# Layer 1 of a two-layer trunk: keys, values and cached keys turned in 32 x 32 blocks by VectorE and placed by DMA

## The chip, the cores and the metric

The kernel runs on one core of one Trainium2 chip. The metric is the device time of one execution in microseconds (us), as the median of several runs. The core's engines work side by side, each through its own queue of instructions in order: TensorE (PE, with its weight loads shown apart as PEld), VectorE (DVE), ScalarE (ACT), GpSimd (POOL) and SyncE (SP). SP computes nothing here; it issues nearly all DMA transfers. An instruction waits at the head of its queue until the semaphores that it needs have come, and everything behind it in that queue waits too.

## What is computed

One inference step of a hybrid encoder trunk with two layers, for a prompt of 512 tokens and a sample of 32 tokens, 1024 wide. Layer 0 mixes tokens with RWKV-7, layer 1 with differential attention. The change is in layer 1, whose part of the reference is, cut down:

```python
h = rmsnorm(x, norm_w)
q, k, v, qm, gate = jnp.split(h @ w_in, [...], axis=-1)      # 12 heads of 128 for q, k and v
k_all = concat([k_past, k]); v_all = concat([v_past, v])     # sample only: 128 cached tokens
def probs(qa, ka):
    s = einsum('bqhd,bkhd->bhqk', qa, ka) * 64 ** -0.5
    return softmax(where(mask, s, NEG_INF))
attn = probs(q1, k1) - lam * probs(q2, k2)
o = einsum('bhqk,bkhd->bqhd', attn, v_all)
out = concat([rmsnorm(o, subln) * c, mem_attention(qm, mk, mv)]) * silu(gate)
return x + out @ w_out, k, v                                 # k and v are outputs too
```

Keys and values are needed in two layouts. The products give them transposed (features on the 128 partitions, tokens along the row). The outputs k and v, and the sum over `attn`, want tokens on the partitions. The cached keys come with tokens on partitions and are needed the other way for the sample's scores.

## The kernel before, in words

Prompt and sample are kept together as 544 columns, in two halves of 272. A main product is a matmul of 128 x 128 weights with 272 columns; weights and activations are split in a high and a low part (`whi`, `wlo`, `hh`, `hl`), so that one output column block of 128 takes 2 halves x 8 slices x 3 = 48 main products into `ps_g`. That is one **block** (`block`, `steps`). Weights come by DMA into five `raw` buffers, two loads for a block, and are split by ACT (`whi`) and DVE (`wlo`) one block ahead.

Layer 1 (`groups`) goes through twelve heads in three groups of four. Each head has a key block, a query block and a value block; after each group come gate blocks, and after the first two groups blocks for the memory's queries. All other work is dealt out among the main products: `block` takes a list of pieces, each with the number (0 to 47) of the main product ahead of which it is issued. The attention of one head is a generator (`diff_head`, `steps` inside it) of 13 pieces, which begin in the head's own value block and end in the next head's key and query blocks (for the group's last head: in a gate block and the block after it). `step(prev, 10, 20, 30, 40, 45)` puts the next five pieces of the previous head at products 10, 20, 30, 40 and 45.

The order within each engine's queue is made when the program is built: of the instructions that are ready at a point, the one that the code issues earlier goes first. In layer 1 no order is written by hand (`self.ordered` is False there).

The pieces of one head are, in order: the split of the keys in high and low (`kh`, `kz`; DMA moves half of `kh` to other partitions); the keys turned and written out; `scores(0)`, `scores(1)`; the sample's scores (`ps_sc`) and `probs(0)`; the values turned and written out; `scores(2)` and `probs(1)`; `weighted(0)`; `scores(3)`; `probs(2)`; `weighted(1)`; `weighted(2)`; `probs(3)`; `weighted(3)`. `scores(t)` makes the scores of 128 prompt tokens and their softmax on DVE and ACT, `probs(t)` turns the probabilities on PE (`ps_aT`), and `weighted(t)` sums t + 1 blocks of values on PE into `ps_o`. That tile comes from a pool of one bank (`psx`), and DVE copies it out to `ot`.

`turned` turns keys or values with four transposes on PE into `ps_kv`, ACT copies them to `kt` or `vt` in SBUF, and one DMA of 256 KB writes the output. For the sample's 32 tokens two more transposes (`ps_kvs`) and an ACT copy give `vs`. Once in a group, four transposes (`ps_ckT`) and an ACT copy turn the cached keys of four heads, which one DMA loaded to `ck`. `diff_end` ends a group: the sample's sums, and its outputs from `vs`. All of these instructions go through a queue object, so that the profile shows line 106 for them; they are told apart by tile.

Of the kernel before, what the change touches and what calls it, by code (L numbers as in the profile page):

```python
# [17 lines left out]
P = 128  # L18
# [90 lines left out]
class Trunk:  # L109
# [238 lines left out]
    def steps(self, w, evac):  # L348

        for v in (slice(0, TH), slice(TH, T)):  # L350
            if len(self.open) > 1:
                self.until(self.open.pop(0))
            ps = self.psg.tile([P, 512], F32, tag="g", name="ps_g")
            for k in range(KT):
                for t, x in ((0, self.hh), (0, self.hl), (1, self.hh)):
                    self.te.matmul(ps[:, :TH], w[t][:, k, :], x[:, k, v], start=k == 0 and x is self.hh and t == 0,
                                             stop=k == KT - 1 and t == 1)
# [1426 lines left out]
    def layer1(self):  # L1784
# [7 lines left out]
        with ExitStack() as ctx:  # L1792
            with ExitStack() as c2:
                self.dfp = p = self.pool("df", 1, ctx=c2)
                m1 = c2.enter_context(ExitStack())
                mp = self.pool("mem1a", 1, ctx=m1, side="right")

                nlam = self.nlam
                self.qs = [p.tile([P, P], F32, name=f"qs{i}") for i in range(2)]
# [98 lines left out]
    def groups(self, w, p, mp, nlam, aside, free):  # L1898

        late = []  # L1900
        for hg in range(3):
# [5 lines left out]
            def gate(c0, pieces):  # L1907
                self.gates += 1
                sg, _, evac = self.gate_evac(self.gates)
                self.block(w, 3 * MIXW + 512 + c0, evac, pieces)  # L1910
                return sg

            for j, (parts, it) in enumerate(heads):
                h = 4 * hg + j
                before = step(prev, 10, 20, 30, 40, 45) if j else late
                k, q, v = parts()
                self.block(w, MIXW + h * P, k, before)
                if not j and hg == 2:
# [12 lines left out]
            fin = lambda j, at: (at, lambda: end.send((j, sgs[j])))  # L1931
            g0 = 4 * hg * P
            sgs.append(gate(g0, step(prev, 10, 20, 30, 40, 45)))
            if hg == 2:
                sgs.append(gate(g0 + P, step(prev, 6, 18, 30, 42)))
                aside()
                sgs.append(gate(g0 + 2 * P, step(end, 2, 10, 18) + [fin(0, 22), fin(1, 36)]))
                sgs.append(gate(g0 + 3 * P, [fin(2, 16)]))
                fin(3, 0)[1]()
                break  # L1940
# [8 lines left out]
                    st["evac"](ps, v)  # L1949
                return evac  # L1950

            self.block(w, 3 * MIXW + st0["c"], query(st0), step(m0, 2) + step(prev, 6, 18, 30, 42))
# [16 lines left out]
    def diff_group(self, hg, p):  # L1969

        a, gr = self.a, {"hg": hg, "on": []}
        gr["ck"] = p.tile([P, 4, P], F32, tag="ck", name="ck")
        gr["cv"] = p.tile([P, 4, P], F32, tag="cv", name="cv")
        gr["ckT"] = p.tile([P, 4, P + TS], F32, tag="ckT", name="ckT")
        gr["vs"] = p.tile([TS, 2, 4, P], F32, tag="vs", name="vs")
        gr["ssb"] = p.tile([P, 2, 160], F32, tag="ssb", name="ssb")
        gr["ss"] = p.tile([P, 3, 16], F32, tag="oss", name="oss")
        return gr

    def cached(self, gr, n):  # L1980

        h = 4 * gr["hg"]
        self.se.dma_start(gr["c" + n][:], self.a["cache_" + n][0, 0, :, h : h + 4])

    def diff_head(self, gr, j, p, nlam):

# [28 lines left out]
            return keys, queries, values  # L2015

        def turned(x, n):
            t = p.tile([P, 4, P], F32, tag="kt" if n == 4 else "vt", name="kt" if n == 4 else "vt", bufs=n - 3)
            ps = self.psm.tile([P, 512], F32, tag="m", name="ps_kv")
            for i in range(4):  # L2020
                self.te.transpose(ps[:, i * P : i * P + P], x[:, i * P : i * P + P], self.ident[:])
            self.ae.copy(t[:], ps[:].rearrange("p (j c) -> p j c", j=4))
            self.se.dma_start(o[n][0, 0, :, h, :].rearrange("(i p) d -> p i d", p=P), t[:])
            return t

        def scores(t):
            n, S = (t + 1) * P, []
# [11 lines left out]
        def probs(t):  # L2039
            n = (t + 1) * P  # L2040
            ps = self.psm.tile([P, 512], F32, tag="m", name="ps_aT")
            for i in range(t + 1):
                self.te.transpose(ps[:, i * P : i * P + P], st["pt", t][:, 0, i * P : i * P + P], self.ident[:])
            st["aT", t] = p.tile([P, 512], F32, tag="aT", name="aT", bufs=2)
# [11 lines left out]
        def steps():  # L2056
# [8 lines left out]
            yield  # L2065
            turned(k, 4)
            if j == 0:
                ps = self.psm.tile([P, 512], F32, tag="m", name="ps_ckT")
                for i in range(4):
                    self.te.transpose(ps[:, i * P : i * P + P], gr["ck"][:, i, :], self.ident[:])  # L2070
                self.ae.copy(gr["ckT"][:, :, :P], ps[:].rearrange("p (j c) -> p j c", j=4))
            self.ae.copy(gr["ckT"][:, j, P:], k[:, TP:])
            yield
            scores(0)
# [8 lines left out]
            yield  # L2083
            if j == 0:
                self.cached(gr, "v")
            st["vt"] = turned(st["v"], 5)
            ps = self.psm.tile([P, 512], F32, tag="m", name="ps_kvs")
            for i, x in enumerate((k, st["v"])):
                self.te.transpose(ps[:, i * P : i * P + P], x[:, T - P :], self.ident[:])
            self.ae.copy(gr["vs"][:, :, j, :], ps[P - TS :, :256].rearrange("p (j c) -> p j c", j=2))  # L2090
# [23 lines left out]
    def diff_end(self, gr, nlam):  # L2114
# [4 lines left out]
        for i, n in ((0, 10), (1, 11)):  # L2119
            self.se.dma_start(o[n][0, 0, :, 4 * hg : 4 * hg + 4, :], vs[:, i])  # L2120
# [5 lines left out]
        aT = p.tile([P, 512], F32, tag="aT", name="aTs", bufs=2)  # L2126
        self.ae.copy(aT[:, :P], ps[:, :P])
        self.ae.copy(aT[:TS, P : 2 * P], ps[:TS, P : 2 * P])
        yield
# [4 lines left out]
                             tile_position=(0, 32 * j))  # L2134
        for j in range(4):
            rj = slice(32 * j, 32 * j + 32)
            self.te.matmul(po[rj, :P], aT[:TS, P + 32 * j : P + 32 * j + 32], vs[:, 1, j, :], start=False, stop=True,
                             tile_position=(0, 32 * j))
        os_ = p.tile([P, P], F32, tag="os", name="os")
        self.ve.tensor_copy(os_[:], po[:, :P])  # L2140
# [32 lines left out]
    def run(self):  # L2173
# [7 lines left out]
        self.ordered, self.later, self.open = False, [], []  # L2181
# [64 lines left out]
```

## Time and profile before

| What | Value |
|---|---|
| Median of 3 runs | 1370.9 us (1369.54 to 1371.71) |
| The profiled execution | 1371.42 us |
| Its span, first to last instruction | 1369.2 us |
| Granted TensorE clock, mean | 0.998 |
| Layer 1's heads and gates in the span | about 800 to 1250 us |
| Work on ps_kv, ps_kvs and ps_ckT | 132 matmuls on PE, 39 copies on ACT |

The times come from one profiled execution. A row of a group reads: line, engine, operation, tile written <- tiles read, shapes, count | busy time in us, mean ns of one | idle time of the engine ahead of them and who ended it. A row of a timeline reads: start in us, length in us, engine, line, operation, tiles, shapes, count. Rows that follow one another closely are merged, with their count at the end. Matmuls are pipelined, so their lengths overlap, and the price of one is read from the starts of its neighbours.

### The profile page before, as it was taken

Reading aid. Unit: us, or ns where it says so; the run is one execution under the profiler, and the core shown is the slowest. Engines: PE = TensorE matmul, PEld = TensorE weight load, DVE = VectorE, ACT = ScalarE, POOL = GpSimd, SP = SyncE. Lnnn points to the kernel's source line nnn. Section 1 sums busy time; section 2 is a strip of 40 time slices with the busy share of each in tenths; the row PEclk is TensorE's granted clock in tenths of the full one; section 3 lists DMA queues with packets and bytes.
Section 4 is the critical chain, followed back from the end, with each engine's and each line's share of the span. In section 5 each row is a group of like instructions: output and inputs, shape, how many; then the busy total and the mean of one; then the engine's idle time right before and its main releaser. Section 6 shows DMA issues by size and latency. Waiting matters only on the chain. (4 is left out here: it accounts for less than half of the span.)

```text
span 1369.2 us, 31861 instructions
## 1 busy us (share of the span) xinstructions
PE 1339.3 (98%) x11845; PEld 1283.9 (94%) x11845; DVE 939.7 (69%) x2353; ACT 822.6 (60%) x2288; POOL 381.9 (28%) x841
## 2 busy tenths in 40 slices
PE   8999999999999999999999999999999999999997
PEld 6988899999999998988999989999999999999997
DVE  5776788888888888667744667775567747667443
ACT  5766777877778777656433466654566537665222
POOL 2138667766686667600000120000000001002000
PEclk9999999999999999999999999999999999999999
DMA  7452322333323332432555563332333323332322
GB/s 224 146 140 70 77 71 57 94 86 74 88 67 84 88 88 64 142 87 76 173 142 147 148 184 88 100 102 82 101 95 94 90 82 94 97 97 79 93 78 73
DMA packets 276964, 139.06 MB, mean 102 GB/s; under 512 B 75769, under 2 KB 265730, under 8 KB 276810
## 3 DMA queue, kind: packets, MB, share of 16 engines
q1 hardware_dynamic: 276746, 137.01, 36.0%
q8 instruction: 94, 1.54, 0.5%
q14 instruction: 60, 0.49, 0.1%
q10 hardware_dynamic: 64, 0.02, 0.0%
HBM read 110.72 MB, written 22.91 MB: 98 GB/s over the span
## 5 line engine op out<-in xcount | busy, mean ns | idle before, releaser
L106 PE MATMUL ps_g<-hh,whi 128*128 128x272 f32 x1808 | 539.7, 299 | 1.0 <-DVE ats L106 0.7
L106 PE MATMUL ps_g<-hh,wlo 128*128 128x272 f32 x1808 | 534.8, 297 | 1.6 <-DVE wlo L106 1.5
L106 PE MATMUL ps_g<-hl,whi 128*128 128x272 f32 x1808 | 532.4, 295 | 0.6 <-DVE hl L106 0.3
L106 PEld LDWEIGHTS ps_g<-hh,whi 128*128 128x128 f32 x1808 | 341.2, 189 | 5.1 <-DVE ats L106 0.9
L106 PEld LDWEIGHTS ps_g<-hh,wlo 128*128 128x128 f32 x1808 | 340.6, 189 | 4.7 <-DVE wlo L106 2.5
L106 PEld LDWEIGHTS ps_g<-hl,whi 128*128 128x128 f32 x1808 | 341.1, 189 | 2.8 <-DVE hl L106 1.3
L106 DVE TENSOR_TENSOR wlo<-raw,whi 128x512 fp32r<-128x512 f32 x314 | 220.1, 712 | 118.3 <-ACT whi L106 114.7
L106 ACT CAST whi<-raw 128x512 fp32r<-128x512 f32 x314 | 188.9, 619 | 115.8 <-PE ps_g L106 62.4
L868 POOL TENSOR_TENSOR tm<-u,m 102x84 f32<-102x84 f32 (+23 forms) x341 | 147.8, 433 | 115.4 <-DMA m<-sc 69.5
L870 POOL TENSOR_TENSOR u<-u,tm 102x84 f32<-102x84 f32 (+23 forms) x341 | 151.6, 445 | 26.6
L106 PE MATMUL ps_g<-hi,wlo 128*128 128x272 f32 x512 | 147.8, 289 | 1.2 <-DVE wlo L106 1.2
L106 PE MATMUL ps_g<-hi,whi 128*128 128x272 f32 x512 | 147.7, 289 | 0.0
L106 PE MATMUL ps_g<-lo,whi 128*128 128x272 f32 x512 | 147.4, 288 | 0.0
L1339 POOL TENSOR_TENSOR lo<-og,hi 128x544 fp32r<-128x544 f32 x8 | 13.2, 1649 | 357.7 <-ACT hi L106 357.2
L106 PEld LDWEIGHTS ps_g<-hi,wlo 128*128 128x128 f32 x512 | 96.4, 188 | 1.7 <-DVE wlo L106 1.6
L106 PEld LDWEIGHTS ps_g<-hi,whi 128*128 128x128 f32 x512 | 96.5, 189 | 0.0
L106 PEld LDWEIGHTS ps_g<-lo,whi 128*128 128x128 f32 x512 | 96.4, 188 | 0.0
L106 ACT ACTIVATE pt<-ps_s,snm 128x128 f32<-128x128 f32 (+3 forms) x96 | 51.0, 532 | 41.7 <-DVE snm L106 41.6
L1763 POOL TENSOR_TENSOR hl<-hn,hh 128x544 fp32r<-128x544 f32 x8 | 12.2, 1536 | 211.4 <-ACT hh L106 211.3
L106 DVE SCALAR_TENSOR_TENSOR SB<-ps_c,dl,sd 64x64 f32<-64x64 f32 x168 | 47.4, 282 | 26.4 <-PE ps_c L106 21.2
L106 ACT COPY sv<-ps_c 64x64 f32<-64x64 f32 x192 | 39.6, 206 | 32.7 <-PE ps_c L106 30.8
L106 ACT ACTIVATE sg<-ps_g 128x272 f32<-128x272 f32 x64 | 25.2, 394 | 41.0 <-PE ps_g L106 38.3
(400 smaller groups left out, 2564.4 us busy)
## 6 DMA issues: line engine op xcount, KB each, us to landing
raw<-in_rw_in_dram SPq DMA_DIRECT2D x114, 256.0 KB
raw<-in_df_in_dram SPq DMA_DIRECT2D x112, 256.0 KB
raw<-in_w_out_dram SPq DMA_DIRECT2D x64, 256.0 KB
oscr<-sg SPq DMA_DIRECT2D x16, 272.0 KB
lo<-oscr SPq DMA_DIRECT2D x16, 272.0 KB
m<-sc SPq DMA_DIRECT2D x33, 128.0 KB
raw<-in_w_mem_v_dram SPq DMA_DIRECT2D x16, 256.0 KB
kh<-kh SPq DMA_DIRECT2D x24, 136.0 KB
```

The lines of the kernel that those rows point to most:

```text
L106: return lambda *a, **k: self.trunk.tie(self, issue(*a, **k))
L868: nc.gpsimd.tensor_tensor(tm[:, :n, :wd], u3[:, :n, kx : kx + 1].to_broadcast(sh), m3[:, kx : kx + 1, kx + 1 :].to_broadcast(sh), ALU.mult)
L870: nc.gpsimd.tensor_tensor(u3[:, :n, kx + 1 :], u3[:, :n, kx + 1 :], tm[:, :n, :wd], ALU.add)
L1339: (self.nc.gpsimd if g % 2 and self.o1 else self.ve).tensor_tensor(lo[:], t, hi[:].bitcast(F32), ALU.subtract)
L1763: nc.gpsimd.tensor_tensor(self.hl[:, k, :], h[:], self.hh[:, k, :].bitcast(F32), ALU.subtract)
```

## The change

DVE's transpose turns each 32 x 32 block of a tile by itself and leaves the blocks where they stand. The change uses it in place of PE's transposes, and lets DMAs put the blocks in place: 32 partitions at a time, in pieces of 32 numbers (128 B).

- **Keys**: one DVE transpose of 128 x 512 into `tb`, then four DMAs of 64 KB straight to the output. The last 32 columns are turned apart into `new`.
- **Values**: the same into `tb`, but four DMAs to a scratch tensor in DRAM (`vscr`, one for odd and one for even heads). Two pieces later (`fetched`) one DMA of 256 KB reads it back as `vt`; after `weighted(0)` another writes `vt` to the output.
- **The sample's keys and values**: from `new`, by four DMAs in a group to `vs` (`samples`) and four to the output.
- **Cached keys**: 16 DMAs, each a block column, in place of one, and four DVE transposes of 128 x 128 into `ckT`.
- **Order**: the pieces stand at products 4, 9, 30, 44 of the one block and 14, 24, 34, 46 of the next. `weighted(0)` moves from before `scores(3)` to after `probs(2)`, at product 14 of the query block; `weighted(1)` stands at 24, `weighted(2)` with `probs(3)` at 34, `weighted(3)` at 46.
- **Held places**: the first main product after a weighted sum may not be put ahead of it in PE's queue (`self.pinned`).
- `aT` has three buffers instead of two.

The diff, cut to its core:

```diff
@@ steps (main products) @@
+                    if self.pinned is not None:
+                        self.order(mm, self.pinned)
+                        self.pinned = None
@@ groups @@
-                before = step(prev, 10, 20, 30, 40, 45) if j else late
+                before = step(prev, 4, 9, 30, 44) if j else late
...
-                self.block(w, h * P, q, step(prev, 6, 18, 30, 42) if j else ())
+                self.block(w, h * P, q, step(prev, 14, 24, 34, 46) if j else ())
@@ cached @@
-        self.se.dma_start(gr["c" + n][:], self.a["cache_" + n][0, 0, :, h : h + 4])
+        if n == "v":
+            self.se.dma_start(gr["cv"][:], self.a["cache_v"][0, 0, :, h : h + 4])
+            return
+        for a in range(4):
+            for j in range(4):
+                r = slice(TS * a, TS * a + TS)
+                self.se.dma_start(gr["ck"][r, j].rearrange("i (b c) -> i b c", c=TS),
+                                  self.a["cache_k"][0, 0, :, h + j, r].rearrange("(b i) c -> i b c", i=TS))
@@ diff_head @@
         def turned(x, n):
-            t = p.tile([P, 4, P], F32, tag="kt" if n == 4 else "vt", name="kt" if n == 4 else "vt", bufs=n - 3)
-            ps = self.psm.tile([P, 512], F32, tag="m", name="ps_kv")
-            for i in range(4):
-                self.te.transpose(ps[:, i * P : i * P + P], x[:, i * P : i * P + P], self.ident[:])
-            self.ae.copy(t[:], ps[:].rearrange("p (j c) -> p j c", j=4))
-            self.se.dma_start(o[n][0, 0, :, h, :].rearrange("(i p) d -> p i d", p=P), t[:])
+            t = p.tile([P, TP], F32, tag="tb", name="kt" if n == 4 else "vb")
+            self.ve.transpose(t[:], x[:, :TP])
+            self.ve.transpose(gr["new"][:, n - 4, j, :], x[:, TP:])
+            to = o[4][0, 0, :, h, :] if n == 4 else self.vscr[h % 2][:]
+            to = to.rearrange("(b i) (a c) -> a i b c", i=TS, c=TS)
+            for a in range(4):
+                r = slice(TS * a, TS * a + TS)
+                self.se.dma_start(to[a], t[r, :].rearrange("i (b c) -> i b c", c=TS))
+
+        def fetched():
+            t = p.tile([P, 4, P], F32, tag="vt", name="vt", bufs=2)
+            self.se.dma_start(t[:], self.vscr[h % 2][:].rearrange("(i p) d -> p i d", p=P))
             return t
+
+        def samples():
+            for a in range(4):
+                r = slice(TS * a, TS * a + TS)
+                self.se.dma_start(gr["vs"][:, :, r], gr["new"][r, 1])
...
-                self.te.matmul(po[:, :P], aT[:, i * P : i * P + P], st["vt"][:, i, :], start=i == 0, stop=i == t)
+                self.pinned = self.te.matmul(po[:, :P], aT[:, i * P : i * P + P], st["vt"][:, i, :], start=i == 0, stop=i == t)
...
-            weighted(0)
-            yield
+            st["vt"] = fetched()
+            if j == 3:
+                samples()
             scores(3)
             yield
             probs(2)
             yield
+            weighted(0)
+            self.se.dma_start(o[5][0, 0, :, h, :].rearrange("(i p) d -> p i d", p=P), st["vt"][:])
+            yield
             weighted(1)
             yield
             weighted(2)
-            yield
             probs(3)
```

More of the change, by code (lines that the diff above doesn't have):

```diff
@@ L355, in steps @@
                 for t, x in ((0, self.hh), (0, self.hl), (1, self.hh)):
-                    self.te.matmul(ps[:, :TH], w[t][:, k, :], x[:, k, v], start=k == 0 and x is self.hh and t == 0,
-                                             stop=k == KT - 1 and t == 1)
+                    mm = self.te.matmul(ps[:, :TH], w[t][:, k, :], x[:, k, v], start=k == 0 and x is self.hh and t == 0,
+                                        stop=k == KT - 1 and t == 1)
+                    if self.pinned is not None:
+                        self.order(mm, self.pinned)
+                        self.pinned = None
                     if k == KT - 1 and t == 1:
@@ L1798, in layer1 @@
                 nlam = self.nlam
+                self.vscr = [self.dp.tile([TP, P], F32, name=f"vscr{i}") for i in range(2)]
                 self.qs = [p.tile([P, P], F32, name=f"qs{i}") for i in range(2)]
@@ L1932, in groups @@
             g0 = 4 * hg * P
-            sgs.append(gate(g0, step(prev, 10, 20, 30, 40, 45)))
+            sgs.append(gate(g0, step(prev, 4, 9, 30, 44)))
             if hg == 2:
-                sgs.append(gate(g0 + P, step(prev, 6, 18, 30, 42)))
+                sgs.append(gate(g0 + P, step(prev, 14, 24, 34, 46)))
                 aside()
@@ L1950, in query @@
                 return evac
-            self.block(w, 3 * MIXW + st0["c"], query(st0), step(m0, 2) + step(prev, 6, 18, 30, 42))
+            self.block(w, 3 * MIXW + st0["c"], query(st0), step(m0, 2) + step(prev, 14, 24, 34, 46))
             sgs.append(gate(g0 + P, step(end, 8, 20, 44)))
@@ L1974, in diff_group @@
         gr["ckT"] = p.tile([P, 4, P + TS], F32, tag="ckT", name="ckT")
-        gr["vs"] = p.tile([TS, 2, 4, P], F32, tag="vs", name="vs")
+        gr["vs"] = p.tile([TS, 4, P], F32, tag="vs", name="vs")
+        gr["new"] = p.tile([P, 2, 4, TS], F32, tag="new", name="new")
         gr["ssb"] = p.tile([P, 2, 160], F32, tag="ssb", name="ssb")
@@ L2067, in steps @@
             if j == 0:
-                ps = self.psm.tile([P, 512], F32, tag="m", name="ps_ckT")
                 for i in range(4):
-                    self.te.transpose(ps[:, i * P : i * P + P], gr["ck"][:, i, :], self.ident[:])
-                self.ae.copy(gr["ckT"][:, :, :P], ps[:].rearrange("p (j c) -> p j c", j=4))
+                    self.ve.transpose(gr["ckT"][:, i, :P], gr["ck"][:, i, :])
             self.ae.copy(gr["ckT"][:, j, P:], k[:, TP:])
@@ L2085, in steps @@
                 self.cached(gr, "v")
[L2086 to L2090, printed above, removed]
+            turned(st["v"], 5)
             st["ot"] = p.tile([P, 4, P], F32, tag="ot", name="ot", bufs=4)
@@ L2118, in diff_end @@
         self.combine(ssb, srs, P + TS, nlam)
-        for i, n in ((0, 10), (1, 11)):
-            self.se.dma_start(o[n][0, 0, :, 4 * hg : 4 * hg + 4, :], vs[:, i])
+        self.se.dma_start(o[11][0, 0, :, 4 * hg : 4 * hg + 4, :], vs[:])
+        for a in range(4):
+            r = slice(TS * a, TS * a + TS)
+            self.se.dma_start(o[10][0, 0, :, 4 * hg : 4 * hg + 4, r], gr["new"][r, 0])
         self.ve.tensor_scalar(ss[:, 1, :], ss[:, 0, :], 1.0 / P, EPS, ALU.mult, ALU.add)
@@ L2180, in run @@
         self.mem, self.out = {}, set()
-        self.ordered, self.later, self.open = False, [], []
+        self.ordered, self.later, self.open, self.pinned = False, [], [], None
         self.place_no = self.acted = 0
```

6 lines of the change are left out of this document (3 added, 3 removed).

## The prediction

> **What bounds the kernel now.** I read the page first, then busy time by window for layer 1, then TensorE's groups with shapes kept apart, then timelines of the stretch around one head.
>
> ```profile
> span 1369.2 us, 31861 instructions
> PE 1339.3 (98%) x11845; PEld 1283.9 (94%) x11845; DVE 939.7 (69%) x2353; ACT 822.6 (60%) x2288; POOL 381.9 (28%) x841
> ```
> ```profile
> 810.00:930.00 120.00, 119.87 (x961) 118.09 (x961) 84.75 (x252) 76.20 (x235) 0.00 (x0) 1.00 0.34 97
> 1141.00:1250.00 109.00, 109.00 (x878) 107.27 (x877) 77.52 (x235) 69.78 (x217) 0.15 (x2) 1.00 0.34 94
> ```
> The columns of the second are length, then busy time of PE, PEld, DVE, ACT and POOL, the granted clock, DMA share and GB/s. In the first and third group of heads PE never rests (119.87 of 120 us, 109.00 of 109) at full clock, while DVE has 71% of its time in use and the DMA engines 34%. In layer 1 time is therefore what PE must issue, plus whatever a change makes it wait.
>
> What PE would shed are these groups:
>
> ```profile
> L106 PE MATMUL ps_kv<-ident,k 128*128 128x128 f32 x48 | 7.2, 272 | 0.0
> L106 PE MATMUL ps_kv<-ident,v 128*128 128x128 f32 x48 | 7.2, 272 | 0.0
> L106 PE MATMUL ps_kvs<-ident,k 128*128 128x128 f32 x12 | 3.3, 273 | 0.0
> L106 PE MATMUL ps_kvs<-ident,v 128*128 128x128 f32 x12 | 3.3, 272 | 0.0
> L106 PE MATMUL ps_ckT<-ident,ck 128*128 128x128 f32 x12 | 1.8, 272 | 0.0
> ```
> That is 48 + 48 + 12 + 12 + 12 = 132 transposes. Their 272 ns is a latency, not a price, since matmuls overlap. The price is read from starts:
>
> ```profile
> 817.78 0.29 PE L106 MATMUL ps_g<-hl,whi 128*128 128x272 f32 x1
> ...
> 819.17 0.29 PE L106 MATMUL ps_g<-hh,whi 128*128 128x272 f32 x1
> 819.30 0.60 PE L106 MATMUL ps_kv<-ident,v 128*128 128x128 f32 x4
> ...
> 819.87 0.37 PE L106 MATMUL ps_g<-hl,whi 128*128 128x272 f32 x1
> 820.08 0.29 PE L106 MATMUL ps_g<-hh,wlo 128*128 128x272 f32 x1
> ```
> Eleven main products take 1.39 us, so one slot is 0.126 us. From 819.17 to 820.08 lie two such slots and six transposes: 0.91 - 0.25 = 0.66 us, or 0.110 us a transpose, entry and exit included.
>
> **The change, part by part.**
>
> *Transposes off PE.* 132 x 0.110 = 14.5 us, all of it on the path, since PE is what ends last there. Nothing else leaves PE: scores, weighted sums and their counts stay.
>
> *Transposes onto DVE.*
>
> ```profile
> L106 DVE STREAM_TRANSPOSE x<-xr x8: 735/738/739, 688.4 to 761.5; 128x544 f32<-128x544 f32 x8
> L106 DVE TENSOR_TENSOR og<-osT,sg 128x32 f32<-128x32 f32 x8 | 1.5, 183 | 0.0
> ```
> A 128x512 one is 512/544 of 738 ns, 0.69 us; for a 128x32 one I take the 0.18 us of the other row; a 128x128 one lies between them, near 0.3. Twelve heads with two long and two short ones, and three groups with four middling ones: 12 x 1.74 + 12 x 0.3 = 24 us, against 67 us that DVE rests in the two windows above alone. ACT loses its PSUM copies at the same time. Free as a total; its place is the question below.
>
> *The weighted sums.* This is the term that I can least pin down. They share one PSUM buffer (psx, one bank), so each waits until DVE has copied out the one before. For one head the trace shows:
>
> ```profile
> 848.76 0.38 PE L106 MATMUL ps_o<-vt,aT 128*128 128x128 f32 x2
> 853.25 0.61 PE L106 MATMUL ps_o<-vt,aT 128*128 128x128 f32 x4
> 855.19 0.83 PE L106 MATMUL ps_o<-vt,aT 128*128 128x128 f32 x6
> ```
> ```profile
> 853.95 0.27 DVE L106 COPY ot<-ps_o 128x128 f32<-128x128 f32 x1
> ...
> 854.73 0.68 DVE L106 TENSOR_TENSOR wlo<-raw,whi 128x512 fp32r<-128x512 f32 x1
> 855.33 0.74 DVE L106 SCALAR_TENSOR_TENSOR pt<-pt,srs 128x512 f32<-128x512 f32 x1
> 855.99 0.68 DVE L106 TENSOR_TENSOR wlo<-raw,whi 128x512 fp32r<-128x512 f32 x1
> 856.60 1.46 DVE L106 TENSOR_TENSOR kz<-k,kh 64x544 fp32r<-64x544 f32 x2
> 858.09 0.29 DVE L106 COPY ot<-ps_o 128x128 f32<-128x128 f32 x1
> ```
> The sum at 853.25 stands ahead of product 6 of the query block, so that block starts at 853.25 - 6 x 0.126 = 852.50. Its copy follows 0.1 us after it ends. The sum at product 18 ends at 856.02, and its copy comes 2.07 us later, because DVE first does work that the code issues earlier: weight split, softmax, the key's low parts, without a gap to 858.06. Today that lag costs nothing, the next sum being 24 products off. The change puts the first sum at product 14, the second at 24, the third at 34, and ties the following main product behind each, so PE can't run on: a late copy becomes a PE wait, with the whole block queued behind it.
>
> Bounds, in heads 1 to 3 of a group (nine in all; a group's last head is followed by gate and query blocks without the key's low parts, where I take no wait): the first sum starts 1.76 us into the block, ends 0.38 later at 2.14; the second is due at 24 x 0.126 + 0.22 = 3.24 (0.11 us for each of the first sum's two matmuls, as for a transpose). Copied at once: no wait. Copied only when the stretch ends, 858.06 being 5.56 us into the block: done at 5.9, wait 2.6 us. Interpolating the lag between product 6 (0.10) and 18 (2.07) gives 1.41 us at 14, copy done at 2.14 + 1.41 + 0.29 = 3.84, wait 0.6. And if the first copy slips in ahead, the second meets the stretch instead: the third sum is due at 34 x 0.126 + 0.67 = 4.95 and waits to 5.9, 0.9 us. I take 0.7 us a head, between the last two: 9 x 0.7 = 6.3 us given back.
>
> *The value's round trip.* SP's queue and its traffic in the same stretch, and a scratch write with its dependent read from layer 0:
>
> ```profile
> 844.00 0.38 ACT L106 COPY v<-ps_g 128x272 f32<-128x272 f32 x1
> ```
> ```profile
> 844.85 1.17 SPq L106 DMA_DIRECT2D raw<-in_df_in_dram  x2
> 846.11 0.46 SPq L106 DMA_DIRECT2D out_dram<-vt  x1
> 855.44 0.37 SPq L106 DMA_DIRECT2D raw<-in_df_in_dram  x1
> ```
> ```profile
> 844.80:845.80 1.00, 1.00 (x11) 1.00 (x10) 0.71 (x2) 0.59 (x2) 0.00 (x0) 1.00 0.00 0
> 847.80:848.80 1.00, 1.00 (x11) 1.00 (x10) 0.76 (x3) 1.00 (x4) 0.00 (x0) 1.00 1.06 312
> 850.30:855.40 5.10, 5.10 (x40) 4.93 (x40) 3.84 (x12) 3.39 (x9) 0.00 (x0) 1.00 0.00 0
> 752.40:753.40 1.00, 1.00 (x10) 1.00 (x9) 0.18 (x1) 0.00 (x0) 0.00 (x0) 1.00 0.73 113
> ```
> ```profile
> 113.54 1.83 SPq L106 DMA_DIRECT2D sc<-at  x4
> 115.47 0.40 SPq L106 DMA_DIRECT2D sc<-ats  x1
> 116.74 2.00 SPq L106 DMA_DIRECT2D sg<-sc  x6
> ```
> V is complete at 844.38 and can be turned by about 846.6, when SP's two loads are out too. Four writes at 0.46 us each: the last starts at 848.0. From the last scratch write to its reader took 116.74 - 115.47 = 1.27 us: the fetch starts at 849.3. Three transfers of 256 KB issued from 844.85 begin to move at 845.8 and are over by 850.3, so one takes 0.95 + 4.5/3 = 2.45 us: v is back at 851.8. The first sum would be due at 852.50 + 1.76, less the 0.88 us that the key block sheds (six transposes, and the first sum itself), 853.4. Spare: 1.6 us, and SP's next load (855.44) comes after it. Hidden, cost 0; uncovered it costs PE microsecond for microsecond in twelve heads. While SP waits for the writes only the output write and a load due 6 us later queue behind.
>
> The Trainium skill, "DMA: Bandwidth & Descriptors", section Specifications, speaks against the change: pieces below 512 B miss line rate. The last window above has 128 B pieces and moves 113 GB/s at a share of 0.73, where 512 B pieces moved 312 at 1.06, so the trace agrees: 1.9 times the engine time a byte. By that rule a head would need some 3 us more of all engines beside at least 18 us of main products (3 x 48 x 0.126), the DMA share going from 34% to at most 51%, which changes no term.
>
> *Cached keys in 16 transfers.*
>
> ```profile
> 803.35 1.28 SPq L106 DMA_DIRECT2D ck<-in_cache_k_dram  x1
> 806.53 1.13 SPq L106 DMA_DIRECT2D kh<-kh  x2
> ```
> ```profile
> 749.42 2.46 SPq L106 DMA_DIRECT2D xr<-in_x_prompt_dram  x4
> 812.71 0.22 PE L106 MATMUL ps_s<-kh,qp 128*128 128x128 f32 x1
> ```
> At 2.46/4 = 0.6 us an issue, 16 last 10 us in place of 1.28. For the first group they lie just ahead of the key's halves (806.53), which the first scores need at 812.71: between 0 and about 4 us once, if the halves go out 8.5 us later. For the other two groups they go into SP's idle time. I take 1 us.
>
> *The rest* (four transfers for the new keys, an aT buffer more, samples by DMA) goes to a queue and to memory that nothing here waits for: 0, the one buffer of turned keys and values being read out in about 4 us (four issues and a landing, by the rows above), while its next user comes 46 products, 5.8 us, later at the earliest.
>
> Sum: -14.5 + 6.3 + 1 = -7.2 us. The profiled execution took 1371.4 us (2.2 us outside its span), 0.5 above the median; 1370.9 - 7.2 = 1363.7 us.
>
> **The rivals.**
>
> *The copies always wait for the whole stretch* (slower). For it: DVE did all earlier-issued work first around 856 to 858, and the first sum ends just as the first split starts. Against it: the copy at 853.95 did slip between two softmax steps. Price: 9 x 2.6 = 23.4 us, -14.5 + 23.4 + 1 = +9.9: 1380.8 us. It decides from 1.5 us a head, (14.5 - 1)/9.
>
> *Full gain*: every copy finds a gap, as the one at 853.95 did, and the first load costs nothing: 1370.9 - 14.5 = 1356.4 us. Against it: 3.3 us without a gap on DVE.
>
> *Placing by DMA is too slow.* Small pieces double the round trip of 5.2 us (846.6 to 851.8) to 10.4; less 1.6 spare, 3.6 us a head, part of it the wait above: 12 x 3.6 = 43, 1370.9 - 13.5 + 43 = 1400 us; it breaks even at 1.1 us beyond the spare time. Against it: five writes of small pieces and their receipt took 3.2 us in layer 0. The Trainium skill, "VectorE: DVE Perf Modes", section The three transpose paths, warns that transposing by a plain DMA's strides is 19 times slower than the crossbar's way; by that it would be far worse than 1400. Here runs of 128 B stay whole, and the trace does not bear out such a factor.
>
> **How the numbers follow.** Forecast 0.36 (waits of 0.3 to 1.2 us a head: 1360 to 1368); whole stretch 0.32; full gain 0.23; slow DMA 0.09. A measurement of this kernel tells 0.2%, 2.7 us, from no change. Faster: 0.34 of the forecast and 0.22 of the full gain, 0.56. Slower: 0.27 of the whole stretch and 0.07 of the slow DMA, 0.34. Within 0.2%: 0.10. The range runs from the full gain, 1356.5, to the whole stretch, 1381; the tail of the DMA rival and a worse stretch are left out.
>
> **What would show it.** Right: no ps_kv, ps_kvs or ps_ckT; 132 matmuls fewer; twelve ps_o first sums without a wait for a DMA; some PE idle ahead of the second or third ps_o of a head, released by DVE's ot, 6 us in sum; ot copies behind kz. Wrong: that idle near 0, or above 13 us; PE or SP waiting on vscr; the first kh transfers several us later; PE's 0.126 us a product changed.

## The result, and the profile after

The changed kernel takes 1400.9 us (median of 4 runs, 1399.2 to 1402.2) against 1370.8 us before on the same chip (4 runs, 1369.5 to 1371.7): a ratio of 1.0220, 95% interval 1.0207 to 1.0232. The forecast was 1363.7 us, with a range to 1381. It was wrong in sign and outside its range: 30 us slower in place of 7 us faster.

The page of the profile after, its first lines:

```profile
span 1400.0 us, 31750 instructions
## 1 busy us (share of the span) xinstructions
PE 1343.5 (96%) x11713; PEld 1278.8 (91%) x11713; DVE 954.1 (68%) x2413; ACT 805.3 (58%) x2249; POOL 378.6 (27%) x841
```

The 132 matmuls are gone (11845 became 11713), and yet PE is busy no shorter: in part because a matmul at a lower clock lasts longer, and in part because short waits lie within the modelled lengths of the matmuls. PE now rests 56.5 us of its span, against 29.9 before. DVE and ACT have no more to do than they had room for. So nothing is overloaded, and something makes PE wait. The windows by stage say where (columns as in the prediction):

```profile
810.00:930.00 120.00, 107.48 (x807) 103.04 (x806) 77.58 (x234) 63.38 (x203) 0.00 (x0) 0.96 0.47 111
833.40:836.80 3.40, 3.40 (x15) 3.40 (x16) 0.29 (x1) 1.20 (x4) 0.00 (x0) 0.50 0.73 144
889.70:893.00 3.30, 3.03 (x13) 3.04 (x14) 0.64 (x2) 0.88 (x3) 0.00 (x0) 0.50 0.98 266
1091.10:1094.40 3.30, 3.27 (x15) 3.30 (x16) 0.29 (x1) 0.98 (x4) 0.00 (x0) 0.50 0.84 233
```

In the first group of heads PE issues 807 matmuls in 120 us where it issued 961, and the granted clock is 0.96, not 1.00. The other three rows are pieces of layer 1 in which the clock stood at 0.50; the trace of before has no such piece there. The waits of PE name the causes (engine and tile that waited <- what ended it: us in total, times, longest):

```profile
PE ps_o L106 <- DMA vt<-vscr: 13.0, 4, 5.6
PE ps_o L106 <- DVE ot L106: 6.6, 5, 1.3
PE ps_saT L106 <- DVE ssb L106: 4.8, 3, 1.6
PE ps_aT L106 <- DVE pt L106: 1.8, 4, 0.9
```

Before, the same list for layer 1 had one wait of 0.4 us. The four longest are for the values' way through DRAM. This is SP's queue in the first head, then in the third:

```profile
822.98 1.96 SPq L106 DMA_DIRECT2D vscr<-vb  x4
827.66 0.39 SPq L106 DMA_DIRECT2D raw<-in_df_in_dram  x1
828.14 1.11 SPq L106 DMA_DIRECT2D kh<-kh  x2
829.43 0.45 SPq L106 DMA_DIRECT2D vt<-vscr  x1
...
880.74 0.46 SPq L106 DMA_DIRECT2D raw<-in_df_in_dram  x1
886.09 0.80 SPq L106 DMA_DIRECT2D out_dram<-new  x2
887.10 0.38 SPq L106 DMA_DIRECT2D vt<-vscr  x1
```

The fetch (`vt<-vscr`) stands behind a weight load and the key's halves in the one, and in the other behind two of the change's own transfers of new keys (`out_dram<-new`). SP did nothing from 881.2 to 886.1, because the one at its head waited for a key that was not there yet. On PE this becomes:

```profile
827.17 0.63 PE L106 MATMUL ps_aT<-ident,pt 128*128 128x128 f32 x4 [0.89 <-DVE pt L106]
833.39 0.79 PE L106 MATMUL ps_o<-vt,aT 128*128 128x128 f32 x2 [5.59 <-DMA vt<-vscr]
...
834.21 0.43 PE L106 MATMUL ps_g<-hh,whi 128*128 128x272 f32 x1
834.44 0.43 PE L106 MATMUL ps_g<-hl,whi 128*128 128x272 f32 x1
834.66 0.43 PE L106 MATMUL ps_g<-hh,wlo 128*128 128x272 f32 x1
```

Two things are to be seen. `probs(3)` (`ps_aT` x4), which the code issues with the third sum, stands directly ahead of the first: the order made at building had already filled a hole there. And behind the stall a main product takes 0.22 us (834.21 to 834.44 to 834.66), not 0.126.

The second sums wait for DVE. In the second head:

```profile
859.40 0.74 DVE L106 SCALAR_TENSOR_TENSOR pt<-pt,srs 128x512 f32<-128x512 f32 x1
860.06 1.28 DVE L106 TENSOR_TENSOR wlo<-raw,whi 128x512 fp32r<-128x512 f32 x2
861.26 1.47 DVE L106 TENSOR_TENSOR kz<-k,kh 64x544 fp32r<-64x544 f32 x2
862.76 0.71 DVE L106 STREAM_TRANSPOSE kt<-k 128x512 f32<-128x512 f32 x1
863.39 0.25 DVE L106 COPY ot<-ps_o 128x128 f32<-128x128 f32 x1
```
```profile
860.75 0.39 PE L106 MATMUL ps_o<-vt,aT 128*128 128x128 f32 x2
...
862.09 0.29 PE L106 MATMUL ps_g<-hh,wlo 128*128 128x272 f32 x1
863.70 0.71 PE L106 MATMUL ps_o<-vt,aT 128*128 128x128 f32 x4 [1.32 <-DVE ot L106]
```

The first sum is ready by about 861.1; its copy comes at 863.39, behind the splits and the new key transpose.

To set the runs side by side I went through layer 1 from one start of a matmul to the next. Matmuls that write the same tile in the same shape have one usual step to the next start (the median in the kernel before); what a step takes over that is put down to the matmul that came late. In us:

| Kernel | Usual steps | Over, in all | at ps_o | at ps_aT, ps_saT | at ps_s | at ps_g |
|---|---|---|---|---|---|---|
| before | 452.8 | 5.6 | 0 | 0.1 | -0.3 | 2.8 |
| after | 439.4 | 51.4 | 24.4 | 11.0 | 5.8 | 7.9 |

So 13.4 us of work left PE, about as forecast, and 45.8 us of waiting and slow clock came in.

### The profile page after: what moved, and what is told of

It is laid out like the page before. It is cut to its first block, busy times and chain, and to the rows that moved or that the text cites. A ratio compares the mean times of both kernels' runs of the same rounds, so it can differ in the third digit from the quotient of the medians.

```text
span 1400.0 us, 31750 instructions
## 1 busy us (share of the span) xinstructions
PE 1343.5 (96%) x11713; PEld 1278.8 (91%) x11713; DVE 954.1 (68%) x2413; ACT 805.3 (58%) x2249; POOL 378.6 (27%) x841
## 5 line engine op out<-in xcount | busy, mean ns | idle before, releaser
L871 POOL TENSOR_TENSOR tm<-u,m 102x84 f32<-102x84 f32 (+23 forms) x341 | 143.2, 420 | 116.5 <-DMA m<-sc 74.9
L106 PE MATMUL ps_o<-vt,aT 128*128 128x128 f32 x240 | 37.9, 291 | 19.6 <-DMA vt<-vscr 13.0
```

The costliest lines, as they stand in the source:

```text
L106: return lambda *a, **k: self.trunk.tie(self, issue(*a, **k))
L871: nc.gpsimd.tensor_tensor(tm[:, :n, :wd], u3[:, :n, kx : kx + 1].to_broadcast(sh), m3[:, kx : kx + 1, kx + 1 :].to_broadcast(sh), ALU.mult)
```

## The experiments

Three theories. **A**: time is lost where the data are late at fixed places: the fetch behind other transfers, the second sums behind DVE, `ps_saT` ahead of the first sum at a group's end, the second scores; the tie itself matters little. **B**: the tie (`self.pinned`) is the main cause, because PE has nothing to go on with while it waits. **C**: DVE, or the small pieces of DMA, are too slow as such. Ratios are to the kernel before, run on the same chip, with 95% intervals.

**No tie.** The three added lines in `steps` are taken out:

```diff
-                    if self.pinned is not None:
-                        self.order(mm, self.pinned)
-                        self.pinned = None
```

> The change without the tie that holds the main product behind each weighted sum. Theory A (the time is lost in PE waits at fixed points of layer 1: the fetch of the values, issued late by SP; second sums behind DVE's earlier-issued work; ps_saT standing ahead of the first sum at a group's end; second scores): the tie alone explains the three waits for ssb and little else, so about 7 us come back, 1394 us. Theory B (the tie is the main cause, since without it PE would run main products during each wait): some 25 us or more come back, 1375 us or less. Theory C (DVE and its small pieces are too slow as such): no more than 2 us, 1399 us.

Measured: 1370.9 us, ratio 0.9993 (0.9984 to 1.0003). This is theory B, and A as I put it falls: removing the tie gives back all 30 us, and no piece of layer 1 runs at half clock any more. The weighted sums of the second head in this kernel:

```profile
858.16 0.49 PE L106 MATMUL ps_o<-vt,aT 128*128 128x128 f32 x2 [0.78 <-DMA vt<-vscr]
...
859.03 0.71 PE L106 MATMUL ps_o<-vt,aT 128*128 128x128 f32 x4
...
860.13 0.94 PE L106 MATMUL ps_o<-vt,aT 128*128 128x128 f32 x6
...
861.61 1.13 PE L106 MATMUL ps_o<-vt,aT 128*128 128x128 f32 x8
```

Counted in main products, the first stands at product 45 of the query block, not 14, and the others follow 4 to 5 products apart, into the next block; most heads begin at 34. Without the tie the order made at building lets the sums stand behind the main products that can run meanwhile. But the 13.4 us of work that PE shed are not gained either: the table's row reads 439.4 of usual steps and 17.5 over, 10.4 of it at ps_o. Of these, 3.0 us stand in the list of waits (1.8 for `vt`, 1.2 for `ot`); the rest are steps late by too little for the list. Packed so close, each sum may meet the bank that the one before has just left; the spread sums and the second bank below bear on that.

**The fetch on another queue.** One line of `fetched`, tie kept:

```diff
-            self.se.dma_start(t[:], self.vscr[h % 2][:].rearrange("(i p) d -> p i d", p=P))
+            self.nc.gpsimd.dma_start(t[:], self.vscr[h % 2][:].rearrange("(i p) d -> p i d", p=P))
```

> The change with one edit: the DMA that fetches the turned values from scratch is issued from GpSimd's queue, which is idle in layer 1, in place of SP's. Theory A (the fetch lands late because on SP it stands behind transfers that wait for something else): the waits of 5.6 and three times 2.7 us of the first sum for vt go, and the stretches at half clock behind them; 14 to 18 us come back, about 1385 us. Theory C (writes of 128 B pieces and the read behind them are slow themselves): the wait for vt stays at 2 us or more in those heads and appears in others; within 3 us of 1401.

Measured: 1388.3 us, ratio 1.0114 (1.0099 to 1.0129), some 13 us of the 30 back. PE's waits in layer 1:

```profile
PE ps_o L106 <- DVE ot L106: 10.3, 10, 1.3
PE ps_o L106 <- DMA vt<-vscr: 2.8, 2, 2.5
PE ps_aT L106 <- DVE pt L106: 1.9, 4, 0.9
PE ps_saT L106 <- DVE ssb L106: 1.6, 1, 1.6
```

The wait for `vt` falls from 13.0 to 2.8 us, with two pieces of half clock left. The fetch is late through what stands ahead of it on SP, not through the size of its pieces. In the heads that now get their values in time the next cause comes up: ten second sums wait for `ot` in place of five.

**A second bank.** The second and fourth sum to a tile of the other PSUM pool, tie kept, first with the fetch on SP:

```diff
-            po = self.psx.tile([P, 512], F32, tag="x", name="ps_o")
+            po = (self.psm if t % 2 else self.psx).tile([P, 512], F32, tag="m" if t % 2 else "x", name="ps_o")
```

> The change with one edit: the second and fourth weighted sum of a head go to a PSUM tile of the other pool, so that the second sum no longer waits until DVE has copied out the first. Theory A (the second sum waits only for that copy, which DVE does behind work issued earlier): the five waits of some 1.3 us go, 8 to 10 us come back, about 1391 us, and the third sum, ten products later, finds the first copy done. Theory C (DVE has too little time left in this stretch): the wait moves to the third sum or to the scores, and less than 3 us come back.

Measured: 1397.7 us, ratio 1.0182 (1.0167 to 1.0197), so about 5 us by the ratios, half of what A said. In its trace the waits for `ot` fell from 6.6 to 1.9 us, but those for `vt` grew from 13.0 to 18.3. The values came no sooner: in the first head the sum begins 16.5 us after they are complete, against 16.4 in the changed kernel. But `ps_aT` and `ps_saT` cost 0.3 us here in place of 11.0 (table below), and a PE that comes sooner waits longer for the same fetch. With both repairs:

> The change, with the fetch on GpSimd's queue and the second and fourth sums in a tile of the other PSUM pool, the tie kept. With the tie every wait of a weighted sum stops PE, so the two repairs should add: the first alone gave 1388, with 10.3 us of waits for DVE's ot left in its trace. Theory A (the waits are separate): 1388 - 10 = 1378 us. Theory C (DVE is too late whatever the bank): the third sum or the probabilities' copy waits in its place, 1384 us or more.

Measured: 1382.2 us, ratio 1.0080 (1.0065 to 1.0095), between the two expectations, nearer to C's. The repairs did not add: 19.4 us over at ps_o remain, with listed waits for `vt` (7.3), `aT` (4.3) and `ot` (1.9). Mending one wait after the other does not bring the tied places of the change back to the time before.

**No tie, and the fetch on the other queue.**

> The change without the tie and with the fetch on GpSimd's queue, places as in the change. With the tie this queue was worth 12.6 us (1388 against 1401). Theory A (untied, the sums stand some 20 products later, behind the values' landing, so that the queue of the fetch no longer matters): as without the tie alone, 1371 us, within 2 us. Rival (the late fetch costs time by itself, on SP's queue or on the DMA engines, tie or not): 1362 us or less.

Measured: 1368.3 us, ratio 0.9975 (0.9965 to 0.9985). A move that was worth 13 us with the tie is worth 2 to 3 without it: a little more than the first expectation, far from the second.

**Spread sums.** Without the tie and with the fetch on GpSimd's queue, two sums go to the query block and two to the value block after it:

```diff
-                self.block(w, h * P, q, step(prev, 14, 24, 34, 46) if j else ())
+                self.block(w, h * P, q, step(prev, 32, 44) if j else ())
...
-                self.block(w, 2 * MIXW + h * P, v, step(it, 6, 16, 28, 40))
+                self.block(w, 2 * MIXW + h * P, v, sorted(step(it, 6, 16, 28, 40) + (step(prev, 12, 22) if j else []), key=lambda x: x[0]))
```

> The change without the tie, with the fetch on GpSimd's queue, and with the four sums of a head spread: two in the query block at products 32 and 44, two in the next value block at 12 and 22. Without the tie alone the run came to the time before, 1371 us, although PE has 14 us less to do: its trace shows the sums packed 4 to 5 products apart behind product 34, each starting late by some 0.2 us, 10 us in all. Theory A (they wait for the PSUM bank and for aT because they stand so close): spread they don't wait, 1371 - 8 = 1363 us. Rival: values or probabilities come late at these places too, or more work in the value block delays the scores: 1369 us or more.

Measured: 1365.7 us, ratio 0.9957 (0.9940 to 0.9974), most of what A said, and faster than before. The first, third and fourth sums now wait for next to nothing (0.4 us in all); the second ones still begin 4.7 us late, for `ot`. Next, the second scores at 32 (`step(it, 6, 16, 32, 42)`), and the fetch right behind the writes:

> As the run before it (no tie, sums spread, fetch on GpSimd's queue), with the fetch issued right behind the writes and the second scores moved from product 28 to 32. Theory A (the second scores wait some 0.45 us a head for the softmax of the first, because PE now reaches them earlier): 5 us less than the run before it, about 1358 us. Rival (the scores' wait only moves on to the sample's scores or to the next block): within 1 us of the run before it.

Measured: 1364.7 us, ratio 0.9957 (0.9942 to 0.9972): no further gain, as the rival has it. The spread run had only 1.8 us over at ps_s, nearly all of it in the heads that open a group: in the others the fourth sum of the head before, at 22, stands between the first and the second scores and gives the softmax its time. The move took 0.9 us of that away, and 1.1 us more appeared at ps_o.

**The tie with other places.** Here the tie is back; the sums stand at 38 and 46 of the query block and 12 and 22 of the value block (`step(prev, 38, 46)`; a group's last head at 34, 38, 42, 46), the fetch on GpSimd's queue right behind the writes.

> With the tie: sums at products 38 and 46 of the query block and 12 and 22 of the next value block (a group's last head: 34, 38, 42, 46), fetch on GpSimd's queue right behind the writes. It tells the tie from the places. Theory A (the tie costs only what the data are late at the place where it holds a sum; here they are mostly in time, but for the first two heads and the last of each group, whose sums stand close): 1364 to 1370 us. Theory B (the tie is harmful as such, PE having nothing to go on with in any short wait): 1380 us or more.

Measured: 1367.5 us, ratio 0.9969 (0.9958 to 0.9980). The same three lines that cost 30 us at the change's places cost about 2 us against the untied spread kernels here, which is within the intervals. But the tie is not in force everywhere. It holds one product behind each sum, not the products after that one. In the first two heads and the last of each group the order made at building lets later products overtake the tied one; in the first head:

```profile
830.56 0.29 PE L106 MATMUL ps_g<-hl,whi 128*128 128x272 f32 x1
830.69 0.28 PE L106 MATMUL ps_g<-hh,whi 128*128 128x272 f32 x1
...
835.60 0.43 PE L106 MATMUL ps_o<-vt,aT 128*128 128x128 f32 x2
835.79 0.37 PE L106 MATMUL ps_g<-hh,wlo 128*128 128x272 f32 x1
```

The product `hh,wlo` that should follow at 830.69 is left out and comes behind the sum, which stands at product 21 of the value block in place of 38 of the query block. In the changed kernel no product leaves its order, and every sum stands where it was put. In the other seven heads the tie holds the sums within a product of where the untied order has them. So B needs its condition: the tie is dear where it holds a sum at a place that its data don't reach in time. At a place that they do reach it costs little; why the tied product is overtaken here and not in the changed kernel stays open.

**Keys alone.** From the kernel before, only the new keys are turned by DVE; values and cached keys stay with PE. The core of the edit:

```diff
+        def keys_out(x):
+            t = p.tile([P, TP], F32, tag="tb", name="kt")
+            self.ve.transpose(t[:], x[:, :TP])
+            self.ve.transpose(gr["new"][:, j, :], x[:, TP:])
...
-            turned(k, 4)
+            keys_out(k)
```

> The kernel before with one part of the change: only the new keys are turned by DVE and placed by DMA; values and cached keys stay with PE and in their old places, without the tie. 60 PE transposes fewer are 6.6 us. Theory A (the keys' part loses some 0.45 us a head at the second scores, whose softmax now starts later against PE, and nothing else): -6.6 + 5.4, about 1369.5 us, no change. Theory C (DVE's transposes delay the rest): 1375 us or more. If the second scores' loss belongs to the new places instead: about 1364 us.

Measured: 1370.7 us, ratio 0.9987 (0.9978 to 0.9997): A's forecast, and with the 5.4 us over at ps_s that A had. The second scores, in the kernel before and in this one:

```profile
839.86 0.29 PE L106 MATMUL ps_g<-hh,whi 128*128 128x272 f32 x1
839.99 0.28 PE L106 MATMUL ps_s<-kh,qp 128*128 128x256 f32 x1
840.11 0.28 PE L106 MATMUL ps_s<-kz,qp 128*128 128x256 f32 x1
```
```profile
838.68 0.29 PE L106 MATMUL ps_g<-hh,whi 128*128 128x272 f32 x1
838.97 0.39 PE L106 MATMUL ps_s<-kh,qp 128*128 128x256 f32 x1
839.19 0.28 PE L106 MATMUL ps_s<-kz,qp 128*128 128x256 f32 x1
```

The first score comes 0.13 us behind the product ahead of it in the one and 0.29 in the other, and the second after 0.12 against 0.22: four transposes of 0.110 us had stood where PE now waits for the first scores' softmax. The wait is too short to be put down to an engine in the list of waits, and it occurs in eleven of the twelve heads. Moving the second scores four products on (`step(it, 6, 16, 32, 42)`):

> The kernel before with the new keys alone turned by DVE and placed by DMA, and the second scores moved from product 28 to 32. With the keys alone the run was 0.9987 of before, 1.3 to 1.8 us, where 60 transposes of PE less are 6.6 us. Theory A (the rest went into the wait of the second scores, 0.45 us a head): the move brings it back, 1371 - 6.6, about 1364.5 us. Rival (the wait moves to the next piece): 1369 us.

Measured: 1366.3 us, ratio 0.9963 (0.9950 to 0.9976). More than half of it comes back; the excess at ps_s is gone, and 2.3 us appear at the values' `ps_kv` transposes, the next piece but one, whose weight loads now wait for ACT's copy of the values (2.4 us in ten waits).

**Together.** No tie, sums at 32 and 44 and at 12 and 22, the fetch on GpSimd's queue right behind the writes, and the second bank:

> No tie, sums spread (32 and 44 of the query block, 12 and 22 of the value block), fetch on GpSimd's queue right behind the writes, second and fourth sums in the other PSUM pool, second scores left at 28. The spread run kept 7 to 8 us of wait ahead of ps_o, most of it 0.55 us a head at the second sum, for DVE's ot. Theory A: with a second bank these go: 1365.7 - 5, about 1361 us. Rival: the waits move to aT or to the bank now shared with ps_aT: 1365 us, or more.

Measured: 1359.6 us (1358.0 to 1361.3), ratio 0.9913 (0.9898 to 0.9928). Its page, and a window of its layer 1:

```profile
span 1357.8 us, 31767 instructions
## 1 busy us (share of the span) xinstructions
PE 1327.2 (98%) x11713; PEld 1270.2 (94%) x11713; DVE 952.8 (70%) x2413; ACT 804.5 (59%) x2249; POOL 388.9 (29%) x853
```
```profile
800.00:930.00 130.00, 129.68 (x1026) 127.03 (x1025) 95.41 (x286) 76.86 (x238) 4.44 (x7) 1.00 0.54 132
```

PE hardly rests (129.68 of 130 us), at full clock, with the same 11713 matmuls as in the change. Next to nothing is left of the late second sums. This is 11.9 us less than before, and 41 less than the change. One more, the group's last head at 30, 36, 42 and 47:

> As the run before it, with the sums of a group's last head at products 30, 36, 42 and 47 in place of 14, 24, 34 and 46. Theory A: the last three waits of some 0.2 us a sum go, 1 to 2 us less than the run before it. Rival: nothing, or the gate blocks' own work waits: within 1 us.

Measured: 1361.9 us, ratio 0.9930 (0.9915 to 0.9945). A miss: 2.3 us slower by the medians, not faster; the intervals overlap. The table, completed:

| Kernel | Usual steps | Over, in all | at ps_o | at ps_aT, ps_saT | at ps_s | at ps_g |
|---|---|---|---|---|---|---|
| no tie | 439.4 | 17.5 | 10.4 | 0.1 | 2.3 | 2.4 |
| fetch on GpSimd's queue | 439.4 | 37.5 | 17.3 | 7.7 | 6.2 | 3.9 |
| second bank | 439.4 | 44.8 | 29.3 | 0.3 | 5.7 | 7.2 |
| both of these | 439.4 | 31.4 | 19.4 | 0.5 | 5.9 | 3.3 |
| no tie, fetch on GpSimd's queue | 439.4 | 16.0 | 8.8 | 0.1 | 2.4 | 2.3 |
| spread, no tie | 439.4 | 13.5 | 7.0 | 0.1 | 1.8 | 2.2 |
| the same, second scores at 32 | 439.4 | 13.7 | 8.1 | 0.1 | 0.9 | 2.3 |
| spread, tied | 439.4 | 15.4 | 7.7 | 0.1 | 2.6 | 2.8 |
| keys alone | 446.7 | 10.2 | 0.2 | 0.1 | 5.4 | 2.1 |
| the same, second scores at 32 | 446.7 | 7.3 | 0.1 | 0.1 | 0.2 | 2.1 |
| together | 439.4 | 7.6 | 1.1 | 0.2 | 1.7 | 2.3 |
| the same, last head at 30 to 47 | 439.4 | 8.3 | 2.1 | 0.2 | 1.8 | 1.9 |

## Why the prediction was wrong, point by point

**Transposes off PE, -14.5 us: right.** By usual steps 13.4 us left PE, and the kernel that waits least gains 11.9. That price of 0.110 us a transpose also fits the keys alone: 60 transposes fewer, 6.1 us less of usual steps.

**Transposes onto DVE, free as a total: right, but their place was not.** They take what was estimated (0.69 us):

```profile
L106 DVE STREAM_TRANSPOSE kt<-k 128x512 f32<-128x512 f32 x12 | 8.5, 709 | 0.3
L106 DVE STREAM_TRANSPOSE vb<-v 128x512 f32<-128x512 f32 x12 | 8.4, 704 | 0.0
```

But `kt` joined the work that DVE does ahead of the first sum's copy, 0.7 us more of the stretch that the second sum waits for. The prediction had costed that stretch from the kernel before, without it. No run takes `kt` out of it alone.

**The weighted sums, 6.3 us: the mechanism right, the size near by luck.** "A late copy becomes a PE wait, with the whole block queued behind it" is what the trace shows. The second sums begin 7.9 us late in all: 1.5 us in each of five heads, in which the copy waited for the whole stretch, the condition of the first rival, and next to nothing in the others. The forecast had 0.7 us in each of nine heads. In the other four of the nine the first sum had already waited for its values; with the fetch on GpSimd's queue ten second sums wait, and they cost 12.1 us. The third sums came free.

**The value's round trip, "Hidden, cost 0": this is the step that failed.** It cost 13.0 us of waits for `vt`, and four of the five pieces at half clock stand at these waits or right behind them. The prediction read from the queue of before that SP's next load "comes after it", and had the fetch issued as soon as the writes were in. In eight heads the fetch went out within 3 us of the writes, and none of these waits for `vt`. In the other four it went out 4.5 to 6.5 us after them, behind transfers that waited for something else: in the first head a weight load and the key's halves, in the third head of each group the change's own writes of new keys, which the prediction priced at 0 under "The rest" because nobody waits for what they write. What was not asked is who stands behind them. In the first head there was a second reason: DVE turned the values 5.2 us after they were complete, behind a softmax (`v` complete at 817.0, `vb` begun at 822.25). The spare time of 1.6 us was too much as well, though that alone cost nothing in the changed kernel: in the five heads with the least in between, the fetch went out 5.1 to 5.8 us after the values were complete (forecast 4.9), and in the four late heads the sum began 2.8 to 4.0 us after the fetch (forecast 2.5). Against the 9.0 us that the forecast had from complete values to the first sum that leaves about 1 us at best, an estimate.

**What the sum did not have.** `ps_saT`, a group's end, ahead of the first sum in PE's queue at a place where DVE has `ssb` 1.6 us later: 4.8 us of waits. The transposes of `probs(3)`, also directly ahead of the first sum: 0.3 to 1.0 us late in each of twelve heads, 5.3 us. The second scores: 5.8 us, about 0.5 in each head. The half clock: the first main products after it take 0.226 us in place of 0.126; over some 18 us at 0.50 in layer 1 (one stretch of 5.0 us behind the longest stall and four of about 3.3) that is about 18 x 0.100/0.226 = 8 us, an estimate; it is contained in the columns of ps_o and ps_g. Of the 37 us between forecast and result the first sums are 13.9, `ps_aT` and `ps_saT` some 11, the second scores some 6 and the second sums 1.6 beyond their term; 5 more stand at ps_g, where much of the half clock is counted.

**Cached keys in 16 transfers, 1 us: it cost less.** No wait of a score for `kh` stands in the list of the changed kernel.

**The rivals.** "Placing by DMA is too slow" gave 1400 us, close to the result, but not by its mechanism: it wanted 3.6 us in each of twelve heads from the transfers' own length, and eight heads show none; another queue for one transfer took 10 of the 13 us away. The spread kernels, with the same small pieces, are faster than before. "Full gain", with 1356.4 us, was missed by 3 us in the best kernel here, and the way there was not better luck in the gaps but other places, another queue and a second bank.

Behind all of these stands a question that the prediction passed over: why the tie was wanted at all. It keeps one main product behind each sum, and in the changed kernel that fixed where the sums stand; but the work on the other engines is ordered by an estimate of when things are ready, and where that estimate has the sum late, DVE's and SP's work is put ahead of what the sum needs. The `ps_aT` found directly ahead of the first sum, and `kt` ahead of `ot`, point to that; the order's estimate itself was not measured.

## What to carry to other kernels

Before you fix an instruction's place in an in-order queue, find out where it would stand without the tie: if the planner puts it 20 products later, ask which input it expects late, since the tie turns any lateness into idle time of the whole queue. For every transfer on a path that must be hidden, list what stands ahead of it in its queue and what each of those waits for; a transfer that nobody reads can still block one that somebody does. And work taken off the bound engine must be re-placed piece by piece: after it is gone, waits that the removed work covered (here the second scores' softmax) come into the open.

## What the runs showed of the hardware

The clock fell after short stalls. In the third head PE did four transposes from 886.87 on, then nothing until the sum at 889.97 (a wait of 2.46 us), and the clock stood at 0.50 from 889.6 to 893.0; in the eighth it had only this:

```profile
1088.17 0.29 PE L106 MATMUL ps_g<-hl,whi 128*128 128x272 f32 x1
1088.90 0.63 PE L106 MATMUL ps_aT<-ident,pt 128*128 128x128 f32 x4 [0.44 <-ACT cmk L106]
1091.13 0.45 PE L106 MATMUL ps_saT<-ident,ssb 128*128 128x128 f32 x1 [1.60 <-DVE ssb L106]
1091.37 0.64 PE L106 MATMUL ps_o<-vt,aT 128*128 128x128 f32 x2
```

A start-to-start gap of 2.2 us, with a wait of 0.44 ahead of it, was followed by 3.4 us at half clock, while gaps of the same kind in the fourth and the twelfth head were not. From the last main product to the sum lie 3.2 us in each of these three heads (the eighth, fourth and twelfth), with five or six transposes in them; whether transposes count as work for the clock no run here tells. The Trainium skill, "TensorE: Matmul & The Clock Gate", Part 1 and "Why this matters for your kernels", names a window of some 3.4 us for both directions and advises against gaps of over about 3 us. The length of the slow stretches agrees (3.41 us, once 6.83); the advice fits the 3.2 us without transposes, and not the gap of 2.2 us. Here such a stretch on a bound PE cost about 1.5 us more than itself, an estimate: 3.41 us x 0.100/0.226.

Writes in pieces of 128 B were no obstacle: from the end of the last issue of the four scratch writes to the issue of the fetch passed as little as 1.5 to 2.1 us in the five heads in which nothing held the fetch up, on SP as on GpSimd's queue (1.8 to 2.9).
